# Expert matmuls in unbroken groups of eight, and the step between gate/up and down in four parts of 128 columns

## The chip, the cores and the metric

One core of a Trainium2 chip runs the whole program; seven cores are idle. The metric is the device time of one execution in microseconds (us), as the median of several runs.

The engines are named as in the profile: PE is TensorE (matmuls, and PEld its weight loads), DVE is VectorE, ACT is ScalarE, POOL is GpSimd, SP issues the weight transfers (DMA).

## The reference

Two transformer blocks of two layers each, on 256 tokens of 1024 features, all in float32. The change touches only the two mixtures of experts of the first block:

```python
for e in range(N_EXPERTS):                       # 16 experts, each 1024 -> 512 -> 1024
    a = jax.nn.silu(hf @ w_gate[e]) * (hf @ w_up[e])
    y = y + combine[:, e:e + 1] * (a @ w_down[e])
```

`combine` is zero but for the two experts that a token is routed to. The second block attends over a context of 256 tokens too; the context's first layer (its attention and its feed-forward net) does not depend on the first block.

## The kernel before, in words

Activations lie feature-major, [128 features, 8 tiles, 256 tokens]. Most weights are used as the exact sum of two float32r parts: a tile of 128x1024 floats (512 KB, a place in the pool `raw`) is loaded by SP, split by ACT (line 356) and DVE (line 357) into places of the pool `hl`, and three matmuls (lines 379 to 381) multiply it.

The experts (`moe_experts`) do without that split: their matmuls are plain float32. Each expert has 64 places for tokens. `gather` collects the tokens of four experts with one-hot matrices into `xg`. `pair` then computes two experts at once, expert j = 0 in PSUM partitions 0 to 63 and j = 1 in partitions 64 to 127, which are the two halves of TensorE's columns. For gate, then for up, it takes four times two tiles of weights (one for each expert) and issues four matmuls of 512 columns on them (line 931): 32 in all. Then ACT makes `ga` = silu(gate) (line 937), DVE multiplies it by up (line 938, 512 columns in one instruction), TensorE transposes it in four blocks of 128 columns (line 941), and ACT copies the transposes to `at` (line 943, 512 columns in one instruction). The down product is 16 matmuls on eight more tiles (line 949), into two PSUM banks `py`. ACT and DVE weigh `py` into `mh` (lines 954, 955), and matmuls in lines 959 and 960 bring the result back to the tokens. There are eight pairs in each of the two layers, so 512 matmuls of line 931 and 256 of line 949.

Weights of the experts come through `load`: of every 12 tiles in the first layer's experts (16 in the second's) four (eight) go to places of the pool `eraw`, the others to the eight places of `raw`, which the other work's weights use too. A tile's place is loaded anew when its last reader is done; SP issues its transfers one after another in a fixed order, so one that waits for its place holds up those behind it.

The experts are not alone: `mix` runs them side by side with another generator (the context's layer in the first stage, more of its feed-forward net in the second), each in proportion to the amounts that it yields. The program's order on each engine is then made by a list scheduler from priorities (the order in which the code was written) and its own idea of when operands are there; on the chip every engine works through that order as it stands. In the order before, the matmuls of `pair` stand among those of the other work.

Of the kernel before, what the change touches and what calls it, by code (L numbers as in the profile page):

```python
# [16 lines left out]
ALU = mybir.AluOpType  # L17
# [3 lines left out]
P = 128  # L21
D = 1024
# [18 lines left out]
# ---------------------------------------------------------------- layout (host)  # L41
# [5 lines left out]
def constants():  # L47
    """Constants that depend on shapes alone: common, of block 1, of block 2, of its even layer."""
# [48 lines left out]
def cols(v):  # L97
    """[n*128] -> [128, n], feature f = n*128 + p."""
    v = np.asarray(v).reshape(-1, P)
    return np.ascontiguousarray(v.T)  # L100


def units(w, mw):
    """[K, M] -> [M/mw, 128, (K/128)*mw]."""
    k, m = w.shape
    a = w.reshape(k // P, P, m // mw, mw).transpose(2, 1, 0, 3)
    return np.ascontiguousarray(a).reshape(m // mw, P, (k // P) * mw)


def kunits(w, kt):  # L110
    """[K, M] -> [K/(128*kt), 128, kt*M]."""
# [5 lines left out]
def modunits(w):  # L117
    """[1024, C] -> [C/2048, 8, 2, 128, 1024]: columns 256*(2j+h).. of four column groups j."""
# [5 lines left out]
def vunits(w):  # L124
    """[1024, M] -> [M/256, 2, 128, 4*256]: halves of the contraction."""
# [20 lines left out]
def layout(i):  # L146
# [28 lines left out]
    # layer A  # L175
# [8 lines left out]
    # modulations  # L184
# [5 lines left out]
    # shared kv  # L190
# [5 lines left out]
    # layer B  # L196
# [5 lines left out]
    # experts  # L202
# [4 lines left out]
    # block 2, even layer: heads in pairs (i of kv head 0, i of kv head 1)  # L207
# [9 lines left out]
    # block 2, odd layer  # L217
# [16 lines left out]
# ---------------------------------------------------------------- the chip  # L234

def mix(*streams):
    """Generators side by side, each (generator, its total of yielded amounts), in proportion."""
# [26 lines left out]
def upto(n, g):  # L264
    """as much of a generator as amounts to n."""
# [8 lines left out]
class Chain:  # L274
    """Generators one after another, for several users: whoever needs the result of one goes on with them."""
# [12 lines left out]
class Net:  # L288
# [9 lines left out]
    # ---- small helpers  # L298
# [4 lines left out]
    def banks(self, es, **kinds):  # L303
        """PSUM banks for each kind of use, beside those of kinds N and L; a kind given as a string shares another's."""
# [21 lines left out]
    def splits(self, es, more, side=None):  # L326
        """more places for the parts of weights."""
# [18 lines left out]
    def wsplit(self, src, kt, mw):  # L346
        """a unit of weights as the exact sum of two float32r parts, [128, kt, mw]."""
# [13 lines left out]
    def ahead(self, *units):  # L361
        """weights split before their turn, each (unit, kt, mw)."""
# [3 lines left out]
    def split_to(self, dh, dl, src):  # L366
        """src (fp32, SBUF or PSUM) as the exact sum of two float32r parts."""
# [3 lines left out]
    def lin(self, w, kt, xh, xl, n, c0=0, kind="L", ps=None):  # L371
        """psum[:, :n] = W[:, c0:c0+128].T @ x, W and x in parts; w a unit, or one for each k; n may be a range."""
# [10 lines left out]

    def lin_t(self, ws, kt, n, xh, xl, t0):
        """psum[128 tokens, n] = x[:, t0:t0+128].T @ W; ws units, each of kt tiles of the contraction."""
# [12 lines left out]
    def values(self, ws, xh, xl, dst, tiles=None):  # L398
        """dst [128, tiles of tokens, 256] = x.T @ W, W in two units of the contraction."""
# [7 lines left out]
    def rsqrt(self, r, v, u):  # L407
        """r = 1/sqrt(v): a guess from v's bits, and three Newton steps; u is scratch."""
# [7 lines left out]
    def rstd_tok(self, sums, nfeat, mul=None, kind="n"):  # L416
        """psum [128 tokens, c] of sums of squares -> [128, c] of 1/sqrt(mean+eps)."""
# [9 lines left out]
    def rms(self, x, kt, scales=(None,)):  # L427
        """sums over features of squares of x [128, kt, 256] times each scale, psums [128 tokens, 2 tiles]."""
# [15 lines left out]
    def spread(self, r, kind="N"):  # L444
        """token-major [128, 2] to all features, psum [128, 256]."""
# [6 lines left out]
    def norm(self, x, kt, g, sc, sh, dh=None, dl=None, keep=None, save=None, late=False):  # L452
        """rms norm of x [128, kt, 256], times g*(1+sc), plus sh; in parts to dh, dl, or whole to keep; late: sc and sh
        come after x."""
# [12 lines left out]
    def normed(self, x, kt):  # L467
        """rms norm of x, without a gain."""
# [6 lines left out]
    def modulate(self, z, ga, sh, dh, dl, eng=None):  # L475
        """z * ga + sh in parts to dh, dl."""
# [11 lines left out]
    def room(self, kt):  # L488
        """[128, 256] for each of kt tiles of features, in the weights' place."""
# [3 lines left out]
    def gains(self, kt, g, sc):  # L493
        """g*(1+sc)."""
# [1094 lines left out]
```

## Time and profile before

| what | value |
|---|---|
| time, median of 3 runs | 2190.9 us (2189.96 to 2191.31) |
| span of the profiled execution, first to last instruction | 2181.0 us |
| the rest of the median, around that span | 9.9 us |
| PE busy | 2045.4 us (94%) |
| DVE, ACT busy | 1194.1 us (55%), 826.0 us (38%) |
| mean DMA rate over the span | 226 GB/s |
| first stage with experts | 327 to 705 us of the span |
| second stage with experts | 979 to 1292 us of the span |

A busy PE is one whose matmuls are under way; matmuls overlap, so what one costs is read from the start of one to the start of the next, not from its duration. In the timeline a float32 matmul of the experts counts as two instructions, so "x2" is one matmul of the program and "x4" two.

### The profile page before, as it was taken

The numbers are of one execution on the slowest core, as the hardware profiler recorded it, in microseconds if no ns is written. First come the engines' busy times: TensorE is split into PE (matmuls) and PEld (weight loads), VectorE is DVE, ScalarE is ACT, GpSimd is POOL, SyncE is SP. The second block draws the span as 40 slices with busy tenths as digits, with TensorE's granted clock in tenths as the row PEclk, the third lists the DMA queues.
The fourth block names the chain that finished last, engine by engine and source line by source line (L and its number), as shares of the span: only waits on it lengthen the run. The fifth ranks groups of instructions, "written<-read, shape, count | busy, mean of one in ns | idle before, by whom it ended". The sixth has DMA issues, their size and how long they took to land.

```text
span 2181.0 us, 35834 instructions
## 1 busy us (share of the span) xinstructions
PE 2045.4 (94%) x13942; PEld 1482.8 (68%) x13942; DVE 1194.1 (55%) x3145; ACT 826.0 (38%) x1532; POOL 138.1 (6%) x152
## 2 busy tenths in 40 slices
PE   5999889999998999989999999997999999998999
PEld 3666654444445877783555448766999877768999
DVE  3644643333244676761233247867777555576776
ACT  2443323333123455541121134665444434444443
POOL 1000200000002020100000013102000100001000
PEclk8999889999999999999999999998999999998999
DMA  9788677758787566447877996302655443324552
GB/s 374 267 304 311 248 261 308 267 214 328 293 347 280 203 224 223 144 166 314 360 287 298 409 359 215 134 21 79 211 184 173 158 145 115 113 102 135 185 186 95
DMA packets 135848, 492.87 MB, mean 226 GB/s; under 512 B 15136, under 2 KB 15536, under 8 KB 135408
## 3 DMA queue, kind: packets, MB, share of 16 engines
q1 hardware_dynamic: 134640, 487.63, 61.4%
q8 instruction: 114, 1.87, 0.3%
q10 hardware_dynamic: 864, 2.53, 0.3%
q0 software_dynamic: 160, 0.27, 0.1%
q14 instruction: 70, 0.57, 0.1%
HBM read 489.32 MB, written 1.05 MB: 225 GB/s over the span
## 4 chain that ended last, share of the span: by engine, by line
PE 49%; DVE 3%; ACT 1%; DMA 1%; issue 1%; POOL 0%; SPq 0%; POOLq 0%; ACTq 0%; DVEq 0%
PE psL L379 8%; PE psL L381 8%; PE psL L380 8%; PE psE L931 6%; PE psE L949 2%; PE psM L556 1%; PE psS L1381 1%; PE psT L636 1%; PE psS L1276 1%; PE psD L379 1%; PE psD L381 1%; PE psD L380 1%; PE psV L614 1%; PE psL L393 1%; PE psL L395 1%; PE psL L394 1%
## 5 line engine op out<-in xcount | busy, mean ns | idle before, releaser
L379 PE MATMUL psL<-hh,H 128*128 128x256 f32 (+1 forms) x1800 | 533.8, 298 | 14.4 <-ACT H L356 6.1
L381 PE MATMUL psL<-hh,L 128*128 128x256 f32 (+1 forms) x1800 | 524.2, 293 | 5.3 <-DVE L L357 5.3
L380 PE MATMUL psL<-hl,H 128*128 128x256 f32 (+1 forms) x1800 | 523.2, 292 | 4.1 <-DVE hl L483 3.8
L357 DVE TENSOR_TENSOR L<-raw,H 128x1024 fp32r<-128x1024 f32 (+1 forms) x336 | 410.3, 1225 | 183.0 <-ACT H L356 181.3
L356 ACT CAST H<-raw 128x1024 fp32r<-128x1024 f32 (+1 forms) x336 | 347.1, 1039 | 390.3 <-PE psL L380 123.1
L379 PEld LDWEIGHTS psL<-hh,H 128*128 128x128 f32 x1800 | 350.0, 195 | 58.1 <-issue 25.3
L381 PEld LDWEIGHTS psL<-hh,L 128*128 128x128 f32 x1800 | 348.4, 194 | 32.0 <-issue 16.4
L380 PEld LDWEIGHTS psL<-hl,H 128*128 128x128 f32 x1800 | 349.2, 194 | 15.4 <-issue 4.5
L931 PE MATMUL psE<-eraw,xg 128*64 128x512 f32 x512 | 155.1, 617 | 8.5 <-PEq L997 8.5
L436 POOL TENSOR_TENSOR sa<-sa,sq 128x256 f32<-128x256 f32 x83 | 76.7, 924 | 1215.7 <-ACT sq L434 1210.0
L931 PE MATMUL psE<-raw,xg 128*64 128x512 f32 x512 | 145.3, 603 | 0.0
L556 PE MATMUL psM<-raw,crep 128*32 128x256 f32 x1408 | 126.2, 408 | 15.9 <-DVE crep L606 13.7
L589 ACT ACTIVATE pr<-psS,nm,hr 128x512 f32<-128x512 f32 (+1 forms) x96 | 67.7, 706 | 100.4 <-DVE nm L583 57.8
L949 PE MATMUL psE<-raw,at 128*64 128x512 f32 x384 | 100.0, 599 | 5.4 <-ACT at L943 5.3
L379 PE MATMUL psL<-ah,H 128*128 128x256 f32 x296 | 87.1, 297 | 4.8 <-DVE x L1165 1.3
L380 PE MATMUL psL<-al,H 128*128 128x256 f32 x296 | 84.3, 285 | 0.7 <-DVE al L369 0.7
L381 PE MATMUL psL<-ah,L 128*128 128x256 f32 x296 | 83.8, 284 | 0.3 <-DVE L L357 0.3
L931 PEld LDWEIGHTS psE<-eraw,xg 128*64 128x64 f32 x512 | 38.7, 139 | 64.7 <-issue 54.0
L580 DVE TENSOR_REDUCE mx<-psS 128x1 f32<-128x512 f32 (+1 forms) x80 | 46.1, 580 | 58.6 <-PE psS L1276 44.4
L556 PEld LDWEIGHTS psM<-raw,crep 128*32 128x32 f32 x1408 | 38.9, 113 | 54.9 <-issue 16.5
L931 PEld LDWEIGHTS psE<-raw,xg 128*64 128x64 f32 x512 | 37.0, 136 | 54.2 <-issue 45.2
L955 DVE SCALAR_TENSOR_TENSOR mh<-psE,wsl,mh 128x512 fp32r<-128x512 f32 x32 | 23.3, 747 | 82.5 <-ACT mh L954 82.0
(404 smaller groups left out, 3474.8 us busy)
## 6 DMA issues: line engine op xcount, KB each, us to landing
raw<-in_mod_dram SPq DMA_DIRECT2D x192, 512.0 KB, 4.8
raw<-in_ed_dram SPq DMA_DIRECT2D x96, 512.0 KB, 8.3
raw<-in_fg_dram SPq DMA_DIRECT2D x66, 512.0 KB, 4.4
raw<-in_fu_dram SPq DMA_DIRECT2D x66, 512.0 KB, 4.2
raw<-in_fo_dram SPq DMA_DIRECT2D x66, 512.0 KB, 4.1
eraw<-in_eg_dram SPq DMA_DIRECT2D x64, 512.0 KB, 7.7
raw<-in_eg_dram SPq DMA_DIRECT2D x64, 512.0 KB, 9.2
raw<-in_eu_dram SPq DMA_DIRECT2D x64, 512.0 KB, 7.6
```

The lines of the kernel that those rows point to most:

```text
L356: nc.scalar.copy(h[:, :n], r[:, :n])
L357: nc.vector.tensor_tensor(l[:, :n], r[:, :n], h[:, :n].bitcast(F32), op=ALU.subtract)
L379: mm(ps[:, ns], wh, xh[:, k, ns], start=k == 0, stop=False)
L380: mm(ps[:, ns], wh, xl[:, k, ns], start=False, stop=False)
L381: mm(ps[:, ns], wl, xh[:, k, ns], start=False, stop=k == kt - 1)
L436: (nc.vector if i else nc.gpsimd).tensor_tensor(acc[i], acc[i], sq, op=ALU.add)
L556: nc.tensor.matmul(ps[32 * j:32 * j + 32, 256 * hf:256 * hf + 256], crep[:, k, :], r[:, 256 * j:256 * j + 256], start=k == 0, stop=k == KD ...
L580: V.reduce_max(mx, ps[:, :n], axis=AX.X)
L589: nc.scalar.activation(p, ps[:, :n], AF.Exp, bias=nm, scale=scale, accum_out=sm)
L931: nc.tensor.matmul(ps[64 * j:64 * j + 64, :], xg[:, 2 * q + k, sl[j]], r[j][:, 512 * k:512 * k + 512], start=q + k == 0, stop=q + k == 4)
L949: nc.tensor.matmul(py[hf][64 * j:64 * j + 64, :], at[:, k, 64 * j:64 * j + 64], r[j][:, 512 * hf:512 * hf + 512], start=k == 0, stop=k == 3)
L955: V.scalar_tensor_tensor(yl[:, fs], py[hf], wsl[:, pr:pr + 1], yh[:, fs].bitcast(F32), op0=ALU.mult, op1=ALU.subtract)
```

## The change

The eight matmuls on four weight tiles are handed to a new helper, `burst`, which issues the first of them with its normal priority and raises that of the seven others by 4000, so that they stand right behind it. The first one uses the tile that is loaded last of the four. A stream now yields 3.6 once for such a group, where it yielded 1.8 twice. Between gate/up and down, product, transpose and copy are issued for 128 columns at a time. The rest of the diff takes out comments and docstrings, and changes nothing in the program.

```diff
+    def burst(self, mms):
+        for i, (o, w, r, start, stop) in enumerate(mms):
+            with self.tc.high_priority(offset=4000 if i else 0):
+                self.nc.tensor.matmul(o, w, r, start=start, stop=stop)
...
             for src in (a["eg"], a["eu"]):
                 ps = self.psum("E")
-                for q in range(4):
-                    r = [load(src[l, 2 * pr + j, q]) for j in range(2)]
-                    for k in range(2):
-                        for j in range(2):
-                            nc.tensor.matmul(ps[64 * j:64 * j + 64, :], xg[:, 2 * q + k, sl[j]],
-                                             r[j][:, 512 * k:512 * k + 512],
-                                             start=q + k == 0, stop=q + k == 4)
-                    yield 1.8
+                for q0 in range(0, 4, 2):
+                    r = {(q, j): load(src[l, 2 * pr + j, q]) for q in (q0, q0 + 1) for j in range(2)}
+                    self.burst([(ps[64 * j:64 * j + 64, :], xg[:, 2 * q + k, sl[j]], r[q, j][:, 512 * k:512 * k + 512],
+                                 q0 == 0 and (q, k) == (1, 1), q0 == 2 and (q, k) == (2, 0))
+                                for q in (q0 + 1, q0) for k in (1, 0) for j in (1, 0)])
+                    yield 3.6
                 gu.append(ps)
             ga = self.t(mo, [P, DE], "ga", bufs=1)
             nc.scalar.activation(ga, gu[0], AF.Silu)
-            tt(ga, gu[1], ga, op=ALU.mult)
             pt = self.psum("E")
+            at = self.t(mo, [P, 4, P], "at", bufs=1)
             for k in range(4):
-                nc.tensor.transpose(pt[:, k * P:(k + 1) * P], ga[:, k * P:(k + 1) * P], self.ident)
-            at = self.t(mo, [P, 4, P], "at", bufs=1)
-            nc.scalar.copy(at, pt.rearrange("p (k s) -> p k s", k=4))
+                ks = slice(k * P, (k + 1) * P)
+                tt(ga[:, ks], gu[1][:, ks], ga[:, ks], op=ALU.mult)
+                nc.tensor.transpose(pt[:, ks], ga[:, ks], self.ident)
+                nc.scalar.copy(at[:, k], pt[:, ks])
             py = [self.psum("E"), self.psum("E")]
-            for k in range(4):
-                r = [load(a["ed"][l, 2 * pr + j, k]) for j in range(2)]
-                for hf in range(2):
-                    for j in range(2):
-                        nc.tensor.matmul(py[hf][64 * j:64 * j + 64, :], at[:, k, 64 * j:64 * j + 64],
-                                         r[j][:, 512 * hf:512 * hf + 512], start=k == 0, stop=k == 3)
-                yield 1.8
+            for k0 in range(0, 4, 2):
+                r = {(k, j): load(a["ed"][l, 2 * pr + j, k]) for k in (k0, k0 + 1) for j in range(2)}
+                ks = (0, 1) if k0 == 0 else (3, 2)
+                self.burst([(py[hf][64 * j:64 * j + 64, :], at[:, k, 64 * j:64 * j + 64],
+                             r[k, j][:, 512 * hf:512 * hf + 512], k == 0, k == 2)
+                            for k in ks for hf in range(2) for j in (1, 0)])
+                yield 3.6
```

**PE, gate of the second pair of the second layer.** Before, each row is one matmul of the program; `psE` is gate's PSUM bank, `raw` a weight tile, and lines 959 and 960 are the end of the first pair.

```order
L931 MATMUL psE_14992<-raw_14993,xg_11720 64x512
L960 MATMUL psN_14894<-SG_11721,mh_11716 128x256
L960 MATMUL psZ_14898<-SG_11721,mh_11716 128x256
L931 MATMUL psE_14992<-raw_14995,xg_11720 64x512
L931 MATMUL psE_14992<-raw_14993,xg_11720 64x512
L959 MATMUL psN_14902<-SG_11721,mh_11716 128x256
L960 MATMUL psN_14902<-SG_11721,mh_11716 128x256
L931 MATMUL psE_14992<-raw_14995,xg_11720 64x512
L931 MATMUL psE_14992<-raw_15001,xg_11720 64x512
```

The same place in the change, with the same work at lines 964 and 965; each tile is used twice, once for each of its two blocks.

```order
L388 MATMUL psE_15046<-raw_15053,xg_11768 64x512
L388 MATMUL psE_15046<-raw_15051,xg_11768 64x512
L388 MATMUL psE_15046<-raw_15053,xg_11768 64x512
L388 MATMUL psE_15046<-raw_15051,xg_11768 64x512
L388 MATMUL psE_15046<-raw_15049,xg_11768 64x512
L388 MATMUL psE_15046<-raw_15047,xg_11768 64x512
L388 MATMUL psE_15046<-raw_15049,xg_11768 64x512
L388 MATMUL psE_15046<-raw_15047,xg_11768 64x512
L964 MATMUL psN_14948<-SG_11769,mh_11764 128x256
L965 MATMUL psN_14948<-SG_11769,mh_11764 128x256
```

Where one or two of the experts' matmuls stood between those of lines 959 and 960, eight stand in a row. Counted over the whole order, the experts' 384 matmuls of each layer stand in 110 (first layer) and 75 (second) unbroken stretches before, and 61 of these 185 hold a single matmul; in the change they stand in 49 and 36, none of odd length, and 16 of the down groups have two matmuls of the same expert behind each other.

**PE, the last pair of the second layer, from up to down.** Before, `ga` is transposed in four blocks (one row, x4) ahead of the 16 matmuls of the down product, whose first rows stand here.

```order
L931 MATMUL psE_16669<-eraw_16696,xg_16138 64x512
L941 MATMUL psE_16705<-cst_64,ga_16702 128x128 x4
L949 MATMUL psE_16712<-raw_16714,at_16710 64x512
L949 MATMUL psE_16712<-raw_16716,at_16710 64x512
L949 MATMUL psE_16713<-raw_16714,at_16710 64x512
L949 MATMUL psE_16713<-raw_16716,at_16710 64x512
L949 MATMUL psE_16712<-raw_16722,at_16710 64x512
```

The same place in the change, up to the first row of the second down group.

```order
L388 MATMUL psE_16759<-eraw_16776,xg_16216 64x512
L947 MATMUL psE_16794<-cst_64,ga_16792 128x128 x2
L388 MATMUL psE_16808<-raw_16812,at_16795 64x512
L388 MATMUL psE_16808<-raw_16810,at_16795 64x512
L388 MATMUL psE_16809<-raw_16812,at_16795 64x512
L388 MATMUL psE_16809<-raw_16810,at_16795 64x512
L388 MATMUL psE_16808<-raw_16816,at_16795 64x512
L388 MATMUL psE_16809<-raw_16816,at_16795 64x512
L388 MATMUL psE_16808<-raw_16814,at_16795 64x512
L388 MATMUL psE_16809<-raw_16814,at_16795 64x512
L947 MATMUL psE_16794<-cst_64,ga_16792 128x128 x2
L388 MATMUL psE_16809<-raw_16828,at_16795 64x512
```

Two transposes now stand ahead of the first down group and two behind it. In eight of the 16 pairs the second down group follows them with nothing between; in the others some of the other work stands there. On SP 16 of some 1,300 transfers stand two to twelve rows earlier or later.

## Rows read from the trace of the kernel before

**Rows 1.** The head of the page.

```profile
span 2181.0 us, 35834 instructions
```

**Rows 2.** The two stages by windows: engines' busy time, PE clock, DMA share, GB/s.

```profile
327.00:705.00 378.00, 363.72 (x1750) 176.74 (x1750) 144.18 (x415) 119.21 (x239) 14.86 (x17) 1.00 0.77 294
979.00:1292.00 313.00, 297.01 (x1481) 144.68 (x1482) 85.91 (x156) 47.87 (x77) 0.00 (x0) 0.99 0.84 334
```

**Rows 3.** Timeline of PE, second stage: start, us, instructions.

```profile
1004.36 0.28 PE L959 MATMUL psZ<-SG,mh 128*128 128x256 f32 x1
1004.57 1.07 PE L931 MATMUL psE<-raw,xg 128*64 128x512 f32 x2
1005.57 0.39 PE L960 MATMUL psN<-SG,mh 128*128 128x256 f32 x1
1005.79 0.28 PE L960 MATMUL psZ<-SG,mh 128*128 128x256 f32 x1
1006.01 1.08 PE L931 MATMUL psE<-raw,xg 128*64 128x512 f32 x4
1007.02 0.39 PE L959 MATMUL psN<-SG,mh 128*128 128x256 f32 x1
...
1008.68 0.28 PE L960 MATMUL psZ<-SG,mh 128*128 128x256 f32 x1
1008.80 0.28 PE L959 MATMUL psN<-SG,mh 128*128 128x256 f32 x1
```

**Rows 4.** Timeline of PE, second stage: four matmuls (0, 0, 1, 1), and eight.

```profile
1086.60 1.95 PE L949 MATMUL psE<-eraw,at 128*64 128x512 f32 x8
1088.47 0.39 PE L381 MATMUL psL<-ah,L 128*128 128x256 f32 x1
...
1215.31 3.65 PE L931 MATMUL psE<-eraw,xg 128*64 128x512 f32 x16
1218.89 0.38 PE L379 MATMUL psL<-ah,H 128*128 128x256 f32 x1
```

**Rows 5.** Timeline between up and down of one pair, idle time in brackets.

```profile
1251.51 0.69 DVE L938 TENSOR_TENSOR ga<-psE,ga 128x512 f32<-128x512 f32 x1 [10.73 <-PE psE L931]
1252.26 0.66 PE L941 MATMUL psE<-cst,ga 128*128 128x128 f32 x4 [0.85 <-DVE ga L938]
1253.01 0.58 ACT L943 COPY at<-psE 128x512 f32<-128x512 f32 x1 [7.84 <-PE psE L941]
1253.64 7.14 PE L949 MATMUL psE<-eraw,at 128*64 128x512 f32 x32 [0.73 <-ACT at L943]
```

**Rows 6.** PE's waits: first stage (two rows), second stage (three): us, times, longest.

```profile
PE psE L941 <- DVE ga L938: 3.7, 6, 0.8
PE psE L949 <- ACT at L943: 2.7, 5, 0.7
...
PE psE L941 <- DVE ga L938: 5.8, 7, 0.9
PE psE L949 <- ACT at L943: 5.3, 8, 0.7
...
PE psN L959 <- DMA eraw<-in_eu_dram: 0.8, 1, 0.8
```

**Rows 7.** Groups by line: products and copies of 256 columns.

```profile
L369 DVE TENSOR_TENSOR al<-sil,ah 128x256 fp32r<-128x256 f32 x66 | 28.1, 427 | 3.3 <-ACT ah L368 3.3
L368 ACT CAST ah<-sil 128x256 fp32r<-128x256 f32 x66 | 26.5, 401 | 34.1 <-DVE sil L1179 34.1
```

**Rows 8.** SP's longest waits, first stage (two rows), second stage (one).

```profile
SPq L335 <- PE psE L931: 98.0, 47, 11.1
SPq L335 <- PE psE L949: 89.6, 43, 11.9
...
SPq L335 <- PE psE L931: 70.2, 36, 14.1
```

**Rows 9.** Windows of 15 us in the second stage, columns as in group 2.

```profile
1024.00:1039.00 15.00, 13.41 (x67) 5.68 (x64) 2.57 (x4) 1.53 (x2) 0.00 (x0) 1.00 0.36 134
1204.00:1219.00 15.00, 15.00 (x82) 7.58 (x82) 5.21 (x9) 2.88 (x4) 0.00 (x0) 1.00 1.03 416
1264.00:1279.00 15.00, 15.00 (x73) 5.63 (x70) 2.91 (x7) 0.60 (x1) 0.00 (x0) 1.00 1.03 418
```

**Rows 10.** An issue of the experts' weights, us to landing.

```profile
raw<-in_ed_dram SPq DMA_DIRECT2D x96, 512.0 KB, 8.3
```

## The prediction, on record before the changed kernel ran

> **What bounds the kernel now.** I read the windows of the two stages first. PE is busy 363.7 of 378 us in the first and 297.0 of 313 in the second, at the full clock (1.00 and 0.99, the 2.4 GHz level); DVE is at 38% and 27%, and the DMA engines at 0.77 and 0.84 of their time [rows 2]. So PE's own queue sets both stages, and the question is what its time is made of. The list of PE's waits says that it hardly stops: 17.5 us in both stages for `ga` and `at`, and 0.8 us for a transfer [rows 6]. SP, on the other hand, waits for PE to give weight places free, 98.0 + 89.6 us in the first stage and 70.2 us in the second for the longest kinds alone [rows 8]: the places are mostly full, and transfers follow PE.
>
> The timeline then shows what a visit of the experts' matmuls among other work costs. One matmul alone starts at 1004.57, and the next other matmul at 1005.57: 1.00 us. Two, one in each half of the columns, take from 1006.01 to 1007.02: 1.01 us [rows 3]. So the halves run side by side, and one matmul alone wastes a half. Eight take 3.58 us (1215.31 to 1218.89) [rows 4], so a step of two costs (3.58 - 1.01) / 3 = 0.86 us. Around a visit more is lost: the last other matmul starts 0.21 us before it (1004.36 to 1004.57), the first after it is followed only 0.22 us later (1005.57 to 1005.79), where such matmuls follow each other in 0.12 us (1008.68 to 1008.80) [rows 3]. A visit of one step thus costs 1.00 + 0.21 + 0.22 - 2 x 0.12 = 1.19 us, of which 0.86 is work and 0.33 is for coming and going.
>
> **The change part by part.**
>
> *Visits.* The order has 110 + 75 stretches of the experts' matmuls before and 49 + 36 in the change: 61 and 39 visits fewer. At 0.33 us that is 20.1 + 12.9 = 33 us. The price was read where float32r matmuls of the full width stand around; beside other shapes it may be 0.25 to 0.5 us, so 25 to 50 us.
>
> *Half-empty steps.* I counted the steps of each stretch as the larger of its two halves' counts: 224 + 211 before, 192 + 192 in the change, where no stretch is odd. 32 and 19 steps fewer at 0.86 us are 27.5 + 16.3 = 44 us. This needs one more fact, since the down groups have two matmuls of one expert behind each other: do they cost a step? In the trace four matmuls in the order 0, 0, 1, 1 took from 1086.60 to 1088.47, 1.87 us, and that is two steps (2 x 0.86 and 0.15 at the end), not three [rows 4]. So they cost none.
> The Trainium skill ("TensorE: Matmul & The Clock Gate", Part 3, what overlaps and what doesn't) says that matmuls start and end strictly in program order. By that rule the four would have taken three steps, and the trace disagrees. Counted so, there would be 445 steps before and 400 in the change, 39 us instead of 44.
>
> *Between up and down.* A product of 512 columns takes 0.69 us on DVE and a copy 0.58 on ACT [rows 5], of 256 columns 0.43 and 0.40 [rows 7]; drawn out to 128 columns by the difference, 0.30 and 0.31. Where PE has nothing else, it waits 0.85 us for `ga` and 0.73 for `at` [rows 5]; these stops came in 13 of 16 pairs [rows 6]. The first wait gets shorter by 0.69 - 0.30 = 0.39, the second by 0.27, but the second product (0.30) now stands ahead of the first group: 0.36 us a pair, 5 us over 13 pairs. Against that, in eight pairs the second group follows the last two transposes with nothing between, and waits for them and two copies: two transposes (half of 0.66 for four [rows 5]) and 2 x 0.31 give 0.95 us, 8 us in all. The two nearly cancel; I take zero, with 5 us of gain and 8 of loss as its bounds. The extra instructions (0.5 us of DVE and 0.7 of ACT a pair) lie on engines that are at 38% or less.
>
> *Four tiles at once.* A group starts only when four tiles have landed, and gives their places free at its end. This is the part that can take the gain back. At the full DMA rate of 416 GB/s [rows 9] a tile of 0.524 MB takes 1.26 us, four take 5.0, while a group takes PE 4 x 0.86 + 0.15 = 3.6. Over a whole stage there is enough: the first moves 378 x 294 GB/s = 111 MB, 267 us at the full rate, against 378 - 48 = 330 us of PE; the second moves 104.5 MB, 251 us, against 313 - 29 = 284. Locally it is not so. By windows of 15 us the DMA share is 0.96 or more in six of 25 in the first stage (90 us) and in eleven of 21 in the second (165 us), five of these in one piece from 1204 to 1279 [rows 9], while between them the DMA engines fall to 0.36 [rows 9]. If nothing were gained in the full windows, 48 x 90/378 + 29 x 165/313 = 27 us would be given back; if the places' contents carry PE over them, as they do now, nothing. I take the middle, 13 us: the last pairs of the second stage surely cannot be faster than their transfers, but the gain falls mostly where other work is mixed in, and there the DMA engines have pauses.
>
> *Sum.* 33 + 44 + 0 - 13 = 64 us. The span falls from 2181 [rows 1] to 2117; with the 9.9 us that lie around it the time is 2190.9 - 64 = 2127 us. What comes after each stage depends on it alone (a norm, then the next layer), so the stages' gain goes through to the end.
>
> **The rivals.**
>
> *All of it stays.* PE is never short of tiles, and visits beside other shapes cost 0.4 to 0.5 us. For it: 0.8 us of waiting for transfers now, and SP's queue waiting for PE. Against it: 75 us at the full rate at the end of the second stage. 77 us at least, up to 44 + 50 = 94: 2097 to 2114.
>
> *The transfers take half.* The groups drain 12 (16) places in steps of four: with one group in work and its places freed together, only two (three) groups are ahead. A freed place's tile takes 8.3 us to land [rows 10], the fourth of a group 3 x 1.26 more, 12.1 us; two groups in between last 7.2 us plus the other work that stands there. Where 1 to 2 us are missing at a third to a half of the 85 stretches, 30 to 60 us go: 2145 to 2180, about 2157.
>
> *Slower: PE waits at every group.* The same mechanism on the other side. There are 96 groups of eight in the two layers; the gain of 77 us is gone when each waits 77 / 96 = 0.8 us longer for its fourth tile. If the rate bound each of them, 5.0 - 3.6 = 1.4 us, 134 us, the time would be 2190.9 + 57 = 2248. For it: landing takes 8.3 us, more than two groups. Against it: the stages' means, which leave 63 and 33 us of DMA time free. Some 2195 to 2250, most likely near its lower end.
>
> *It does nothing.* PE's work in the stages could be bound by something that moves with it: the other work's chains on ACT and DVE, in whose shadow the experts' matmuls then stand. Then PE would show the same stages with more waits, 2191. Against it: the stops listed now sum to 17.5 us of 691 [rows 6], so PE nearly always has an instruction whose operands are there.
>
> **How the numbers follow.** The forecast (56 to 80 us less, 2110 to 2138) gets 0.50, all of it staying 0.17, half taken back 0.19, no change 0.04, slower 0.10. A measurement of this kernel can tell 0.2%, 4 us, from no change; so faster is 0.50 + 0.17 + 0.19 = 0.86, the same 0.04, slower 0.10. The predicted time is 2127 us. The range leaves out the slower case and the outermost of the others: 2099 to 2170.
>
> **What would show it.** The windows of the stages: they should last about 337 and 290 us. The timeline: groups as x16 that take 3.6 us, then a group of other work. PE's waits: a few us each for `at` at the second down group, and waits for DMA (or for the tiles' names) of some 10 us in sum, most of them in the second stage's last third; DMA share of the second stage above 0.9. If waits of PE for transfers sum to over 30 us, the second rival is right; if they are under 3 us and the stages still last over 345 and 300 us, my price of a visit or of a half-empty step was wrong. I would be wrong altogether if the group's matmuls did not run two at a time, which 3.6 us for x16 settles.

## The result, and the profile after

The changed kernel took 2157.6 us (median of 4 runs, 2154.3 to 2163.8) beside 2190.4 us before (2188.9 to 2191.3): a ratio of 0.9859, 95% interval [0.9846, 0.9871]. By the ratio that is 31 us less, by the medians 33. I had forecast 64 us less; the time lies inside the range (2099 to 2170), but by the ratio under half of the forecast gain came. The profiled execution of the change took 2154.3 us, 1.8 us more than its span, and in the later runs it is 1.8 or 1.9 too. So most of the 9.9 us that I put around the span of before is something else: that profile shows an execution some 8 us faster than the median (an estimate), and the two spans differ by 28.5 us, less than the medians.

The head of the changed kernel's page, and its two stages by windows, beside [rows 1, 2] (the first again from 327 us on, and both ending about as far behind the experts' last matmul as there):

```profile
span 2152.5 us, 35957 instructions
```

```profile
327.00:688.00 361.00, 333.69 (x1760) 175.53 (x1760) 150.50 (x440) 123.50 (x263) 13.68 (x18) 0.99 0.80 308
962.00:1261.00 299.00, 279.16 (x1478) 143.68 (x1478) 88.26 (x179) 54.50 (x103) 0.00 (x0) 0.99 0.89 351
```

The stages last 361 and 299 us where I expected 337 and 290. In these windows PE stands still (their length less PE's busy time) for 27.3 + 19.8 = 47 us, and before for 14.3 + 16.0 = 30 us. The timeline of PE in the first stage shows that the groups themselves do what I said: eight matmuls (x16) from 336.29 to 339.87, 3.58 us as in [rows 4].

```profile
336.29 3.65 PE L388 MATMUL psE<-raw,xg 128*64 128x512 f32 x16
339.87 0.70 PE L1281 MATMUL psS<-kc,ah 64*128 64x256 f32 x2
340.50 3.65 PE L388 MATMUL psE<-raw,xg 128*64 128x512 f32 x16
344.08 0.70 PE L1281 MATMUL psS<-kc,ah 64*128 64x256 f32 x2
```

What is new stands in the list of PE's waits, here the changed kernel's first stage (us, times, longest), beside [rows 6]:

```profile
PE psS L1281 <- ACT pr L595: 4.0, 3, 1.7
PE psE L947 <- ACT at L948: 3.0, 8, 0.5
PE psZ L642 <- ACT pt L645: 2.9, 5, 0.7
PE psZ L964 <- DVE x L966: 1.9, 7, 0.3
PE psN L964 <- DVE x L966: 1.9, 4, 0.5
PE psN L964 <- ACT mh L959: 1.8, 3, 0.8
PE psE L388 <- DMA raw<-in_eu_dram: 1.2, 1, 1.2
PE psE L388 <- ACT at L948: 1.1, 3, 0.4
```

and its second stage:

```profile
PE psE L947 <- ACT at L948: 4.6, 12, 0.5
...
PE psN L964 <- ACT mh L959: 2.7, 2, 1.8
PE psE L388 <- ACT at L948: 2.1, 6, 0.4
PE psN L964 <- DVE x L966: 1.9, 6, 0.5
```

Transfers are almost absent (1.2 us). Many small stops have come up instead: transposes that wait for the copy before them (line 947), result matmuls that wait for DVE to empty their bank (line 964), and the other work's softmax (lines 1281, 642), for which PE hardly stopped before. The first stage of before lists, under its own line numbers, only these for the softmax and for a bank that DVE has to empty:

```profile
PE psS L1276 <- ACT pr L589: 0.4, 1, 0.4
PE psN L959 <- DVE x L961: 0.3, 1, 0.3
```

To see what they cost with all that lies around them, I took from the trace, for every PE instruction of the two stages (from the experts' first matmul to 9.5 us after their last), the time from its start to the next one's start, and sorted it by what the two are. "Experts" is from one of their matmuls to whatever follows; "into" from another matmul into theirs; "`ga`" is all that starts or ends at a transpose of `ga`; "other" is between two matmuls of the other work (the pairs' result matmuls are among these), and those of them in which PE stood still for over 0.02 us are listed apart, whole, with their number. A last matmul of the experts ahead of a transpose counts under `ga`. Visits and steps are counted in the order, as in the prediction. All in us, both stages together.

| kernel | visits | steps | experts | into | `ga` | other, running | other, with a stop | sum |
|---|---|---|---|---|---|---|---|---|
| before | 185 | 435 | 400.8 | 39.8 | 34.1 | 204.5 | 11.0 (17) | 690.2 |
| the change | 85 | 384 | 344.3 | 14.3 | 48.4 | 213.5 | 35.6 (54) | 656.1 |
| e1, groups of 8, old step | 76 | 384 | 358.2 | 15.8 | 27.5 | 213.1 | 39.3 (57) | 653.9 |
| e14, groups of 8, two banks | 81 | 384 | 350.6 | 15.3 | 32.9 | 213.0 | 40.3 (59) | 652.1 |
| e3, groups of 4, four parts | 137 | 384 | 348.2 | 23.0 | 44.8 | 207.8 | 28.6 (44) | 652.4 |
| e12, groups of 4, old step | 121 | 384 | 358.6 | 23.8 | 31.7 | 208.1 | 28.9 (45) | 651.1 |
| e16, groups of 4, two banks | 128 | 384 | 355.9 | 23.6 | 32.3 | 207.6 | 28.2 (44) | 647.6 |
| e13, groups of 2, old step | 134 | 384 | 352.9 | 28.1 | 33.0 | 208.3 | 20.9 (32) | 643.2 |
| e15, groups of 2, two banks | 137 | 384 | 352.5 | 25.9 | 32.9 | 208.1 | 21.7 (33) | 641.1 |

From before to the change, "experts", "into" and "other, running" fall by 56.5 + 25.5 - 9.0 = 73 us; stops in the other work take back 24.6 and the transposes 14.3. That leaves 34 us. Outside the stages 4.8 us are lost (1.8 ahead, 0.3 between, 2.7 behind them), and 0.8 comes from where the table cuts its last step: the spans differ by 28.5.

Two of these columns need a closer look. Of the 24.6 us PE stood still for 14.2; the rest is the running time of the matmuls ahead of the stops, part of which would have been spent without a stop too. And in the `ga` column PE stood still no longer than before, 16.2 us against 16.8; there the running time rose, since the transposes stand in 44 separate stretches in place of 17.

### The profile page after: what moved, and what is told of

The parts are those of the page before. It is cut to its first block, busy times and chain, and to the rows that moved or that the text cites. A ratio compares the mean times of both kernels' runs of the same rounds, so it can differ in the third digit from the quotient of the medians.

```text
span 2152.5 us, 35957 instructions
## 1 busy us (share of the span) xinstructions
PE 2000.3 (93%) x13942; PEld 1483.6 (69%) x13942; DVE 1203.1 (56%) x3193; ACT 835.4 (39%) x1580; POOL 134.2 (6%) x152
## 4 chain that ended last, share of the span: by engine, by line
PE 49%; DVE 3%; DMA 1%; ACT 1%; issue 1%; POOL 0%; POOLq 0%; SPq 0%; ACTq 0%; DVEq 0%
PE psL L379 9%; PE psL L380 8%; PE psL L381 8%; PE psE L388 8%; PE psM L562 1%; PE psS L1386 1%; PE psT L642 1%; PE psS L1281 1%; PE psD L379 1%; PE psD L381 1%; PE psD L380 1%; PE psV L620 1%; PE psL L399 1%; PE psL L401 1%; PE psL L400 1%
## 5 line engine op out<-in xcount | busy, mean ns | idle before, releaser
L379 PE MATMUL psL<-hh,H 128*128 128x256 f32 (+1 forms) x1800 | 534.7, 299 | 14.3 <-ACT H L356 4.3
L388 PE MATMUL psE<-eraw,xg 128*64 128x512 f32 x512 | 122.6, 624 | 9.5 <-PEq L1002 9.5
L388 PE MATMUL psE<-raw,xg 128*64 128x512 f32 x512 | 116.0, 597 | 1.3 <-DMA raw<-in_eu_dram 1.2
L388 PE MATMUL psE<-raw,at 128*64 128x512 f32 x384 | 89.0, 601 | 2.1 <-ACT at L948 2.1
L379 PEld LDWEIGHTS psL<-ah,H 128*128 128x128 f32 x296 | 56.7, 193 | 13.9 <-DVE ctx L1170 4.7
```

Source lines behind the costliest of these rows:

```text
L379: mm(ps[:, ns], wh, xh[:, k, ns], start=k == 0, stop=False)
L388: self.nc.tensor.matmul(o, w, r, start=start, stop=stop)
```

## The experiments

Two theories stood at first. "Cover": the groups give PE's whole gain, but the experts' scattered matmuls used to fill the time in which short chains on DVE and ACT ran, and these chains now stand bare. "Transfers": four tiles at once make PE wait for places and rate. Each time is the median of 4 to 11 runs beside the kernel before on the same chip; the ratio is that to before.

### One part alone, and the size of the group

`e1_groups_only` undoes the step in four parts, `e2_four_parts_only` has that step alone, in the kernel before. The edit of the first (the second is the same in the other direction; where `at` is made is left out):

```diff
-            for k in range(4):
-                ks = slice(k * P, (k + 1) * P)
-                tt(ga[:, ks], gu[1][:, ks], ga[:, ks], op=ALU.mult)
-                nc.tensor.transpose(pt[:, ks], ga[:, ks], self.ident)
-                nc.scalar.copy(at[:, k], pt[:, ks])
+            tt(ga, gu[1], ga, op=ALU.mult)
+            for k in range(4):
+                nc.tensor.transpose(pt[:, k * P:(k + 1) * P], ga[:, k * P:(k + 1) * P], self.ident)
+            nc.scalar.copy(at, pt.rearrange("p (k s) -> p k s", k=4))
```

> The groups of eight with the old step between up and down (product, copy of 512 columns, four transposes in a row). Cover theory (the groups give the whole gain on PE's own time, and new waits of PE for short chains on DVE and ACT take more than half of it back, because lone matmuls of the experts used to fill them): the four-part step costs about 3 us net (transposes 7.0 us dearer on PE, waits 3.6 us shorter) and the order has 9 visits fewer than the change, 3 us, so about 2151 us against 2157.6 of the change. Four-part theory (the step in four parts is what takes the gain back): about 2130. Transfer theory (groups that need four tiles at once wait for transfers): no difference from the change, 2157.

> The matmuls as before, only the step between up and down in four parts of 128 columns. The order has 212 visits and 448 steps instead of 185 and 435: 27 x 0.33 + 13 x 0.86 = 20 us. Cover theory: that and some 3 us for the transposes, so 2205 to 2215 us against 2190. Four-part theory: above 2220. Transfer theory says nothing of it.

e1: 2153.8 us, ratio 0.983 [0.9817, 0.9843]; e2: 2202.7, 1.0057 [1.0043, 1.0072]. The groups alone do slightly more than the whole change, and the four parts alone lose 12 us, in an order with more visits (122 and 90) and steps (448) than before.

`e3_groups_of_four` keeps the four parts and halves the groups (two tiles, four matmuls):

```diff
-                    r = {(q, j): load(src[l, 2 * pr + j, q]) for q in (q0, q0 + 1) for j in range(2)}
+                    r = [load(src[l, 2 * pr + j, q]) for j in range(2)]
...
-                                for q in (q0 + 1, q0) for k in (1, 0) for j in (1, 0)])
-                    yield 3.6
+                                for k in (1, 0) for j in (1, 0)])
+                    yield 1.8
```

> Unbroken groups of four matmuls over two tiles, with the four-part step. Steps as in the change (384), visits 137 instead of 85, 17 us more by their price. Cover theory: twice as many pieces to fill the chains with, so PE's idle time in the two stages falls from 42 us to about 30 and the time is about as in the change, 2153 to 2165. Transfer theory: two tiles at once instead of four, so the 13 us that I had put down for transfers come back, and with the visits it is about 2160 too, but PE's waits for transfers must be seen to fall. If neither holds and only visits count, 2175.

2152.0 us, 0.9828 [0.9813, 0.9843]: 52 visits more than the change, which at 0.33 us would cost 17 us, and yet some 6 us faster. That was the first sign that my price of a visit is not what a visit costs, though this run also asks for two tiles at a time where the change asks for four.

### Transfers, with the order held

`e4_half_the_bytes` loads only half of each expert tile, and both blocks of a tile multiply that half:

```diff
-            return self.wload(src)
+            return self.wload(src[:, :512], 512)
...
-        self.nc.sync.dma_start(r, src)
+        self.nc.sync.dma_start(r[:, :512], src[:, :512])
...
-                             r[k, j][:, 512 * hf:512 * hf + 512], k == 0, k == 2)
+                             r[k, j][:, :512], k == 0, k == 2)
```

> The change with half of each of the experts' weight tiles loaded (columns 0 to 511), which both blocks then use; so the output is not the reference's. The scheduler sees shorter transfers and makes an order of 95 visits instead of 85 (3 us dearer), 384 steps. Cover theory: transfers cost the change 3 us at most, so 2155 to 2163. Transfer theory: 13 to 30 us faster than the change, 2130 to 2145.

2127.7 us, 0.9724 [0.9707, 0.9741], 30 us less than the change. It looked like a proof of "transfers", but the list scheduler, which knows the size of a transfer, had also made another order. The next three take the two apart: the order of one kernel with the bytes of the other, by rewriting the transfers' lengths after the order is made (left out here: the matmuls' operands, as in e4, and the helper `resize`).

```diff
         tile_net(tc, a, out, stop)
+    resize(nc, 512)
```

> The changed kernel with its order on every engine kept instruction for instruction, but each transfer of an expert tile brings only columns 0 to 511 (half its bytes), and both blocks of a tile multiply these same columns; so the experts' result is another. The run with half the bytes before this one gained 30 us against the change, but also had another order (53 and 42 visits). Theory 'cover' (the waits of PE come from short chains on DVE and ACT that stand together): bytes alone give little, 2152 to 2158 us, and PE's idle time in the stages stays about 40 us. Theory 'transfers' (places and rate hold PE up): 2127 to 2135 us, idle time about 25 us.

> The order of the run with half the bytes, instruction for instruction, but every expert tile is transferred whole (both blocks still multiply columns 0 to 511, so the experts' result is another). Theory 'cover': the other order was what gained, 2128 to 2138 us. Theory 'transfers': the order is made for tiles that land sooner than they do, so PE waits for transfers: 2155 to 2165 us, and waits for DMA of over 10 us in the list of PE's waits.

> The kernel before with its order kept, and half of each expert tile's bytes, as in the first run of this call (the experts' result is another). If transfers hold up only groups of eight, it stays within 6 us of before, 2184 to 2191 us; if they hold up both kernels alike, it gains as much as the changed kernel does by half the bytes. Theory 'transfers' expects the first, 2184 to 2191, beside a gain of over 20 us in the changed kernel; theory 'cover' expects little in both.

e5, the change's order with half the bytes: 2155.5 us, 0.9848 [0.9834, 0.9861]; e6, the order of e4 with whole tiles: 2168.5, 0.9906 [0.9891, 0.9921]; e7, the order of before with half the bytes: 2186.5, 0.9994 [0.9985, 1.0003]. In the change's own order half the bytes give nothing that can be told from the change, and in that of before nothing either. The windows of e5, over the same stretches as the change's, say it at a glance: DMA share 0.51 and 0.58 in place of 0.80 and 0.89, and as much PE work in the same time.

```profile
327.00:688.00 361.00, 336.64 (x1761) 176.33 (x1761) 150.16 (x440) 123.49 (x263) 13.88 (x18) 0.98 0.51 174
962.00:1261.00 299.00, 277.77 (x1480) 144.12 (x1480) 89.90 (x182) 53.84 (x103) 0.00 (x0) 0.99 0.58 199
```

So transfers do not hold the change up, to within the intervals of some 3 us. e6 shows that they can: e4's order, which counts on tiles that land sooner, loses some 40 us with whole tiles, partly to waits for them, 9.4 us in both stages in place of e4's 2.0 (here the first stage of e6):

```profile
PE psS L1281 <- ACT pr L595: 6.9, 2, 6.6
PE psE L388 <- DMA raw<-in_eu_dram: 5.4, 2, 3.0
PE psE L947 <- DVE ga L946: 5.2, 1, 5.2
...
PE psE L388 <- DMA raw<-in_eg_dram: 1.7, 1, 1.7
```

Another part is the granted clock, 0.96 and 0.97 in e6's stages where e4 has 0.98 and 0.99: taking the missing share of the clock times the stages' lengths, at most some 14 us, an estimate.

What e4's order is worth while tiles are short, 28 us beside e5, can be read with the sorting of the table. With the same bytes and the same groups of eight (95 visits in place of 85), e4 has 13.0 us of stops in the other work (19 of them) where e5 has 35.4 (53), and all other columns together are alike, 621.6 and 621.5 us; some 5 us more lie between the stages. So groups of eight do not open the stops by themselves: between these two runs it is the order of the work around them that decides.

### The pairs' own chains

`e8_results_two_to_a_bank` was to let four results be under way in place of two:

```diff
-                ps = self.psum("NZ"[k % 2])
+                if k % 2 == 0:
+                    ps = self.psum("NZ"[k // 2 % 2])
+                pk = ps[:, S * (k % 2):S * (k % 2) + S]
```

> The changed kernel, with the sixteen result matmuls of a pair in half banks of PSUM, two results to a bank, so that four results can be under way where two could be; visits and steps of the experts stay as in the change (49 and 36, 384). Theory 'cover': the stops of these matmuls for DVE to empty their bank go (1.9 + 1.9 us listed in the first stage, 3.0 + 1.1 us in the second, some 29 stops, each with 0.27 us of edges): 8 us and up to 8 us of edges, 2142 to 2150 us. Theory 'transfers': these stops only stand where PE would have waited anyway, 2154 to 2160 us.

2158.6 us, 0.986 [0.9842, 0.9879], with the same stops as the change; two lines of its first stage (line 966 is here the change's 964):

```profile
PE psZ L966 <- DVE x L968: 1.9, 7, 0.3
PE psN L966 <- DVE x L968: 1.9, 4, 0.5
```

The run does not test what it was meant to: in the order, a result in the second half of a bank still waits for DVE to have read the first half, so no more results were under way than before.

`e9_short_chains`, `e10_short_chains_half_bytes` and `e11_before_short_chains` cut the DVE and ACT operations of a pair to a quarter of their columns, from the second pair of each layer on, and again after the order is made:

```diff
...
+    short(nc, {941: 1, 946: 4, 948: 4, 959: 2, 960: 2, 966: 8})
     return nc
```

> The changed kernel, its order on every engine and its transfers kept, but from the second pair of each layer on the DVE and ACT operations of a pair's own chains (silu, product, copies of the transposes, the weighing of py, the adding of results to x) work on a quarter of their columns, so that each is shorter; the experts' result is another. The waits of PE for these chains sum to 11 us in the first and 17 us in the second stage of the change (about 75 waits, each with some 0.27 us of edges beside it). Theory 'cover' (PE stands idle for chains that the lone matmuls used to cover): about half of the wait and a third of the edges go, 18 to 25 us, 2130 to 2140 us. Rival 'the next wait' (PE would then wait for other things, tiles or the other stream): 2148 to 2156 us.

> As the run before this one, and with half of each expert tile's bytes in the same order. If transfers become the next bound once the chains are short, it lies over 6 us below the run before; if they don't, within 4 us of it. Theory 'cover': within 4 us, 2128 to 2140. Rival 'the next wait': 2130 to 2142 beside a run before of 2148 or more.

> The kernel before with its order kept, and the same operations of a pair cut to a quarter of their columns (another result). It lists 22 us of waits for its own chains (about 36 waits). Theory 'cover': it gains less than the changed kernel does by the same cut, 8 to 14 us, 2176 to 2182 us, since the experts' scattered matmuls cover its results' chains. If it gains as much or more (2165 to 2172), own chains don't explain where the gain of the groups went.

e9: 2142.4 us, 0.9789 [0.9775, 0.9803]; e10: 2141.6, 0.9782 [0.9767, 0.9797]; e11: 2174.0, 0.9934 [0.9921, 0.9947]. The cut is worth 15 us by the ratios in the change and 14 in the kernel before, so shortening a pair's own chains helps both alike, and that speaks against "cover" as I had put it for these chains; e9 itself lies between the ranges of the two theories. The test is a weak one. In e9's first stage the adding to `x` still takes 283 ns on a quarter of the columns, where 256 take 479:

```profile
L966 DVE SCALAR_TENSOR_TENSOR x<-psN,m,x 128x64 f32<-128x64 f32 x28 | 7.9, 283 | 11.9 <-PE psN L965 11.9
...
L966 DVE SCALAR_TENSOR_TENSOR x<-psN,m,x 128x256 f32<-128x256 f32 x4 | 1.9, 479 | 0.3 <-PE psN L965 0.2
```

So the cut left most stops in being: those in the other work fall only from 35.6 to 31.0 us. Half the bytes add nothing (e10): with short chains transfers are not the next bound.

### Visits against stops

`e12_groups_of_four_old_step` is e3 with the old step.

> Groups of four over two tiles, with the old step of 512 columns between up and down: 72 and 49 visits, 384 steps. Nothing but the price of a visit (0.33 us, 36 visits more than the change): 2169 us. Theory 'cover' (visits are cheap where they fill a wait; the four-part step's lone transposes cost 3 to 4 us): 2145 to 2151 us, the fastest version with whole tiles.

2148.3 us, 0.9818 [0.9803, 0.9832], inside the range of "cover". `e13_groups_of_two` is e12 with one thing changed: it holds only the two matmuls of a step together, so that no step is half empty but the scheduler may put other work after each (the edit for gate and up; that for down is alike):

```diff
+                    for k in (1, 0):
+                        self.burst([(ps[64 * j:64 * j + 64, :], xg[:, 2 * q + k, sl[j]], r[j][:, 512 * k:512 * k + 512],
+                                     (q, k) == (0, 1), (q, k) == (3, 0)) for j in (1, 0)])
+                    yield 1.8
```

> Old step of 512 columns, and only the two matmuls of one step held together (one for each half of the columns): 384 steps as in the change, but 78 and 56 visits against the 46 and 30 of groups of eight with the old step (2153.8 us). By my price of a visit, 0.33 us, 58 visits more cost 19 us: 2173 us. Theory 'cover' (a visit taken away opens as much waiting in the other work as it saves in coming and going): 2146 to 2153 us.

2140.0 us, 0.9784 [0.9768, 0.9799]: where my price of a visit asked for 19 us more than e1, it takes some 10 us less (by the ratios), below the ranges of both theories. Its windows, and its waits of the first stage that answer to those of the change:

```profile
327.00:680.00 353.00, 333.72 (x1752) 170.38 (x1752) 144.26 (x415) 118.77 (x239) 13.33 (x17) 0.99 0.81 313
955.50:1249.00 293.50, 277.57 (x1485) 140.50 (x1486) 87.71 (x159) 50.20 (x81) 0.03 (x1) 0.99 0.90 355
```

```profile
PE psN L962 <- DVE x L964: 1.4, 4, 0.4
...
PE psZ L642 <- ACT pt L645: 0.8, 2, 0.6
PE psZ L962 <- DVE x L964: 0.5, 2, 0.3
...
PE psL L620 <- ACT pt L645: 0.4, 1, 0.4
...
PE psS L1279 <- ACT pr L595: 0.2, 1, 0.2
```

The stops for `x` (line 962 here) sum to 1.9 us in place of 3.8, those for `pt` to 1.2 in place of 2.9, those for `pr` to 0.2 in place of 4.0. The timeline of e13 shows what stands there now: a step of two and matmuls of lines 379 and 381 between one pair of result matmuls and the next.

```profile
420.60 0.28 PE L962 MATMUL psN<-SG,mh 128*128 128x256 f32 x1
420.72 0.28 PE L963 MATMUL psN<-SG,mh 128*128 128x256 f32 x1
420.93 1.08 PE L388 MATMUL psE<-eraw,xg 128*64 128x512 f32 x4
421.94 0.39 PE L381 MATMUL psL<-hh,L 128*128 128x256 f32 x1
422.16 0.28 PE L379 MATMUL psL<-hh,H 128*128 128x256 f32 x1
422.28 0.28 PE L962 MATMUL psZ<-SG,mh 128*128 128x256 f32 x1
```

### The transposes' bank

The timeline of the change's last pair, from its first down group on (idle time in brackets, rows of other engines left out):

```profile
1249.37 3.70 PE L388 MATMUL psE<-raw,at 128*64 128x512 f32 x16
...
1253.01 0.33 PE L947 MATMUL psE<-cst,ga 128*128 128x128 f32 x1
1253.37 0.27 ACT L948 COPY at<-psE 128x128 f32<-128x128 f32 x1 [3.63 <-PE psE L947]
1253.69 0.33 PE L947 MATMUL psE<-cst,ga 128*128 128x128 f32 x1 [0.35 <-ACT at L948]
1254.06 0.27 ACT L948 COPY at<-psE 128x128 f32<-128x128 f32 x1 [0.42 <-PE psE L947]
1254.37 3.65 PE L388 MATMUL psE<-raw,at 128*64 128x512 f32 x16 [0.35 <-ACT at L948]
```

The second transpose waits for the copy of the first, 0.68 us from one to the next (1253.01 to 1253.69): all four go to one tile `pt`, one PSUM bank, and the program lets none start before the copy ahead of it is done. `e14_change_two_banks`, `e15_groups_of_two_two_banks` and `e16_groups_of_four_two_banks` use two banks by turns:

```diff
-            pt = self.psum("E")
+            pt = [self.psum("E"), self.psum("E")]
...
-                nc.tensor.transpose(pt[:, ks], ga[:, ks], self.ident)
-                nc.scalar.copy(at[:, k], pt[:, ks])
+                nc.tensor.transpose(pt[k % 2][:, ks], ga[:, ks], self.ident)
+                nc.scalar.copy(at[:, k], pt[k % 2][:, ks])
```

> The change, with the four transposes of a pair by turns in two PSUM banks, where the change has all four in one, and each transpose but the first there waits until ACT has copied the one before it. 48 and 33 visits. If this wait is what the four-part step costs (the change shows 20 such stops of 7.6 us in sum, and the transposes with their edges take 14 us more than before): 2146 to 2153 us. If the stops only move: 2154 to 2160.

> Groups of two, and the four-part step with its transposes in two banks: 80 and 57 visits. Theory 'cover' and a cheap two-bank step: 2140 to 2150 us. By the price of a visit: 2170 us or more.

> Groups of four over two tiles, and the four-part step with its transposes in two banks: 77 and 51 visits. Beside groups of four with one bank (2152.0 us) and with the old step (2148.3 us): 2144 to 2150 us if the stops of the transposes for each other's copies were the cost of the four parts, 2150 to 2155 if not.

e14: 2153.0 us, 0.9837 [0.9821, 0.9853]; e15: 2139.0, 0.9779 [0.9762, 0.9795]; e16: 2147.5, 0.9811 [0.9796, 0.9827]. By the ratios the second bank gives some 5 us in groups of eight and 4 in groups of four (beside e3), both within intervals that overlap, and four parts with two banks are no better than the old step (e13 and e15; e12 and e16) beyond the intervals. In e14's first stage three of the eight stops are left:

```profile
PE psE L947 <- ACT at L948: 0.9, 3, 0.4
```

The `ga` column falls by 15.5 us, of which 7.9 are stops, and the transposes stand in 29 stretches in place of 44. But stops elsewhere and the experts' column rise by 11 (4 of these are matmuls that the change books under `ga`): what a stop took on PE is only partly given back when it goes. e15 and e13 are the fastest of the versions that do the whole work, 48 and 47 us under the kernel before.

## Why the prediction was wrong

**Half-empty steps, 44 us: about right in size.** "Experts", "into" and "other, running" together fell by 73 us in the change, where this term and the next came to 77. In e13, with 51 visits and 51 steps fewer than before, they fell by 55.8 us, where my prices give 51 x 0.86 + 51 x 0.33 = 61. In e1 and e12 they fell by only 58.0 and 54.6, where the prices give 80 and 65; most of what is missing is a lower granted clock, stops and the booking under `ga`, which together make 15 and 9 us of the "experts" column there (the clock's part, 8 and 3 us, is an estimate). And the down groups with two matmuls of one expert behind each other cost no step: the group at the head of the rows of the last pair above, of that kind, took from 1249.37 to 1253.01, 3.64 us. By the rule of the Trainium skill ("TensorE: Matmul & The Clock Gate", Part 3) that matmuls start and end strictly in program order it would have been a step more, an estimated 4.4 us; the trace disagrees with it here as in [rows 4].

**Visits, 33 us: the step that failed.** The 0.33 us for coming and going were there to be saved, but a visit also covers. I had read its price where PE had other work ready on both sides [rows 3]; in the change PE stops 54 times in the other work in place of 17, for 24.6 us more, a quarter of a microsecond for each of the 100 visits taken away. Of 33 us some 8 stay, or 19 if only the 14.2 us of standing still are counted against them. The runs show it by the size of the groups: with the same 384 steps and the old step, 76, 121 and 134 visits leave 39.3, 28.9 and 20.9 us of such stops (22.3, 15.1 and 11.8 of standing still), and the kernel gets faster with more visits. Between the last two only the number of matmuls held together differs; between the first two the loads and the amounts yielded differ too. The clock adds to it: e1's granted clock is 0.98 in both stages, e13's 0.99, which makes some 6 of the 14 us between them by an estimate from these means. But no fixed price of cover follows: e4, with 95 visits, has 13.0 us of such stops, so they belong to an order and not to a number of visits. The clause that I set down for it came true in its main part: waits for transfers under 3 us and the first stage above 345 us (the second ended at 299, just under its bound) meant a wrong price of a visit. "It does nothing" named the right mechanism, chains of ACT and DVE that stand in the visits' shadow; I gave it little since the stops then listed were few, and that was the mistake: the list shows the stops that there are, not those that the work to be moved keeps away.

**Between up and down, 0 with bounds of -5 and +8: outside the bounds on PE.** By the trace the `ga` column rose by 14.3 us. The waiting came out as I had it, near nothing in sum (16.8 us before, 16.2 in the change), though by another way: I took the transposes between the first and the last to run side by side with the copies, and in the change a transpose often waits for the copy of the one before it (line 947 in the two lists of waits, 20 stops of 7.6 us), while the old waits got shorter. What was missing is the coming and going of the transposes themselves, in 44 stretches in place of 17, where 3.7 us of the rise are only matmuls of the experts booked there. In the time the price is smaller, 6 us (e1), or 5 by e14, whose interval overlaps that of the change.

**Four tiles at once, 13 us: nothing that can be told.** e5 and e7 settle it: in neither order do transfers set the time beyond the intervals. "The transfers take half" forecast about 2157 us, and that is where the time lies, but for a reason that was not there: that it hit was luck.

The sum with what was measured: 73 - 24.6 - 14.3 - 4.8 = 29 us, the difference of the spans to 0.8 us.

**What stays open.** Groups of another size bring another order as a whole, so the price of cover is a mean over the places of one order; which single chain loses it was not isolated (e8 missed, and e9 with e11 speak weakly against the pair's own). No run holds everything but the place of the groups, so that the experts' scattered matmuls covered the chains is argued from the stops' sums and their number, not shown by itself. Nor is it known whether an order as good as e4's exists for whole tiles.

## What to carry to other kernels

Price a stretch of work that is to be moved away not only by its edges but by what would wait if it weren't there: look on the other engines for chains that run under it. Take the part of a grouping that removes real work (here the half-empty steps, by groups of two) and leave the scheduler free for the rest: 2140 us against 2154 with groups of eight and the same step. Judge a grouping by the order that it brings, and not by its size alone: e4 has groups of eight and few stops. When a smaller size makes a kernel faster, hold the order and change the size alone before blaming the size.

## What the runs showed of the hardware

A group right behind short stops ran at half the clock. In the change's second stage the results at 1199 to 1201 us came with three stops (0.87, 0.28 and 0.46 us), and the group of eight right after took 5.28 us (1201.34 to 1206.62) in place of 3.58: the granted clock, 1.00 until then, was 0.65 in the mean of the first 1.7 us and 0.50, the 1.2 GHz level, in the next 2. That the stops brought it about is what the order in time suggests; no run took them away by themselves.

```profile
1199.16 0.39 PE L964 MATMUL psN<-SG,mh 128*128 128x256 f32 x1 [0.87 <-ACT mh L959]
...
1199.95 0.39 PE L965 MATMUL psN<-SG,mh 128*128 128x256 f32 x1 [0.28 <-DVE mh L960]
...
1200.91 0.38 PE L964 MATMUL psN<-SG,mh 128*128 128x256 f32 x1 [0.46 <-DVE x L966]
...
1201.34 5.35 PE L388 MATMUL psE<-eraw,xg 128*64 128x512 f32 x16
1206.62 0.39 PE L964 MATMUL psZ<-SG,mh 128*128 128x256 f32 x1
```

```profile
1199.20:1201.30 2.10, 1.36 (x6) 0.86 (x6) 1.57 (x3) 0.00 (x0) 0.00 (x0) 1.00 1.03 423
1201.34:1203.00 1.66, 1.66 (x7) 0.67 (x8) 0.48 (x1) 0.00 (x0) 0.00 (x0) 0.65 1.04 420
1203.00:1205.00 2.00, 2.00 (x6) 0.49 (x4) 0.00 (x0) 0.00 (x0) 0.00 (x0) 0.50 1.01 410
```

Operations of 128 columns took 284 ns on DVE (line 946) and 265 on ACT (line 948) in the first stage, near my 0.30 and 0.31 us.
